# A two-block transformer kernel: its modulation products issued four at a time, one in each 32-column quarter of the array

## The chip, the cores and the metric

The kernel runs on one core of a Trainium2 chip. Its time is the device time of one execution in microseconds (us); the median of several runs is compared. Five engines work side by side, each through its own instructions in order, and wait for one another through semaphores: TensorE (PE in the profile; its weight loads are shown apart as PEld), VectorE (DVE), ScalarE (ACT), GpSimd (POOL) and SyncE (SP), which here only issues DMA transfers. Some DMAs are issued from ScalarE's queue as well.

## The reference

Two model blocks run one after the other on 256 tokens of 1024 channels, two layers each. The first is a mixer of four branches (a recurrence, a latent attention, a convolution, a cross attention), merged with gates. The second is a block with feed-forward, attention and feed-forward in each layer. Each of its six sublayers is modulated: two conditioning vectors `c` and `c_ctx`, one for each of two token streams, are taken through silu and multiplied with a large matrix, which gives nine rows of 1024 values a layer (shift, scale and gate of each of three sublayers):

```python
h = modulate(rms_norm(x, g_pre), shift, scale)    # h * (1 + scale) + shift
x = x + weight * gate * rms_norm(sublayer(h), g_post)
# shift, scale, gate: parts of  silu(c) @ w_mod + b_mod,  w_mod [1024, 9 * 1024] a layer
```

The modulation rows depend on `c` and `c_ctx` alone, so they can be worked out at any time before the sublayer that reads them. All arithmetic is in float32. The large products are made of three passes in float32r (a 12-bit high and a low part of each operand); the modulation products are plain float32.

## The kernel before

All weights are streamed from DRAM once, in tiles of 128 x 1024 float32 (512 KB). Each tile comes into a pool `wr` of four buffers (line 241) by a DMA on SyncE's queue. `wload` (lines 180 to 192) issues the DMA, lets ScalarE cast the tile to its high part `wh` (line 177) and VectorE subtract to get its low part `wl` (line 178); these two have three buffers each. A `wr` buffer is free again once VectorE has read it. TensorE then multiplies the two parts with the activations: 24 matmuls a weight tile (8 pieces of the contraction, 3 passes), of 256 columns in the first block and of 512 in most of the second. All matmuls are recorded under line 169, all transposes under line 172, so they are told apart by tiles: `ac`, `rw` and `sm` are PSUM banks of the products, `md` is the one bank of the modulation.

The modulation is worked out by a generator, `mods` (lines 1155 to 1201), that runs in the background: `wload` ends with `tick` (line 216), which takes each background generator one step further, that is, up to its next `yield`. In layer 1 of the first block `mods` makes the rows of the first sublayer at one step a tick (line 360). In the second block it makes the other five sublayers at one step every second tick (line 1227, `MODS_TICKS`). The attention adds ticks of its own at each pair of heads, six in the first token stream and two in the second (`HEAD_TICKS`, line 57), between the scores of that pair and the values of the one before; there is no weight tile between these, so modulation steps follow one another.

A sublayer takes six blocks of 512 columns, each over a contraction of 1024. A block is four steps and a fifth. In each of the four, one tile of the modulation matrix is fetched into a `wr` buffer, used by TensorE as it is, without cast, and given back:

```python
for i in range(4):
    ...
    for k in range(2):
        kk = 2 * i + k
        g = 32 * (kk % 4)
        self.mm(ps[g : g + 32], self.cs[:, kk], raw[:, 512 * k : 512 * k + 512], kk < 4, kk >= 4)
    yield
```

The stationary operand `cs` is 128 x 32 (two conditioning vectors and 30 columns of zeros), so a product fills one 32-column quarter of the array and leaves its result in 32 partitions of the bank. Piece `kk` of the contraction goes to quarter `kk % 4`: a step with even `i` uses quarters 0 and 1, one with odd `i` quarters 2 and 3. Each product is recorded as two matmuls and two weight loads, so a step is four matmul records. In the fifth step ScalarE copies the bank into a `wr` buffer (line 1173), and two small DMAs carry the rows to DRAM; after six blocks the four quarters are added and the result is brought into the form that the sublayers read (lines 1178 to 1201).

The framework draws up the order of each engine's instructions when the kernel is built: by the order in which they were issued, but work that it holds ready can be put ahead of work that it expects to wait. Buffers of a pool are given out from those that are free.

Of the kernel before, what the change touches and what calls it, by code (L numbers as in the profile page):

```python
# [9 lines left out]
F32 = mybir.dt.float32  # L10
# [6 lines left out]
PSUM = bass.MemoryType.PSUM  # L17
# [4 lines left out]
S = 256  # L22
W = 512
T = 512
# [28 lines left out]
RWKV_STEPS = ((2, 1), (2, 1))           # by layer and duo  # L53
RWKV_GAPS = (2, 3, 3, 2, 1, 4)
CONV_STEPS, CONV_GAP, XQ_GAP, MLA_GAPS = 3, 2, 1, (2, 1)
MODS_TICKS = 2                          # ticks a step
HEAD_TICKS = (6, 2)                     # ticks at a pair of heads, by stream
HEADS_AHEAD = (0, 1)                    # pairs whose values wait, by stream
EVS = 5                                 # buffers
COLS = ((0, 1), (1, 2), (3, 2), (5, 2), (7, 1))     # row tiles that are transposed at a time  # L60
# [99 lines left out]
class Build:  # L160
# [6 lines left out]
    # -- building stones --  # L167
# [6 lines left out]
    def split(self, h, l, src, eng=None):  # L174
        """src = h + l exactly, h and l with the 12 significant bits of float32r"""
        nc = self.nc
        nc.scalar.copy(h, src)  # L177
        (eng or nc.vector).tensor_tensor(out=l, in0=src, in1=h.bitcast(F32), op=ALU.subtract)  # L178
# [15 lines left out]
    def gemm(self, out, sa, sb, KT):  # L194
        """out = sum over k of a^T b, three float32r passes; sa(k), sb(k) give (high, low)"""
# [7 lines left out]
    def rsqrt(self, out, in_, n):  # L203
        """out = in_ ** -0.5 (exact to float32 rounding), [p, n]"""
        p = in_.shape[0]
        self.nc.gpsimd.tensor_tensor(out=out, in0=in_, in1=self.mhalf[:p, :n], op=ALU.pow)  # L206
# [9 lines left out]
    def tick(self):  # L216
        """a step of the work that is spread over the stream of weights"""
# [17 lines left out]
    # -- the whole --  # L235
    def build(self):
        nc, tc, ap = self.nc, self.tc, self.ap
        with ExitStack() as st:
# [15 lines left out]
            # what the end of the first block needs on the one side, the rest of it and then the second on the other  # L254
# [7 lines left out]
    # ================= first block =================  # L262
    def first(self, fin, st):
# [3 lines left out]
        self.ts = fin.enter_context(tc.tile_pool(name="ts", bufs=4))     # a few columns  # L267
        p1 = self.p1 = pool("p1", 1)
        self.f4 = fin.enter_context(tc.tile_pool(name="f4", bufs=7))     # [128, 1024]
# [9 lines left out]
        self.t1 = pool("t1", 2)     # [128, 256] scratch  # L279
        self.t2 = pool("t2", 2)     # [128, 512] scratch  # L280
        self.d2 = pool("d2", 16)    # [128, 512], four heads of the recurrence
        self.d4 = pool("d4", 5)     # [128, 1024]
        self.rp = pool("rp", 1)     # its diagonal blocks
# [5 lines left out]
    def trig(self):  # L289
        """cos and sin of positions * inv_freq, [token, tile, 16]"""  # L290
# [27 lines left out]
        # the quotient may be off by one either way  # L318
# [63 lines left out]
    def params(self, l):  # L382
        """the small weights of a layer"""
# [4 lines left out]
        # halves and the like, worked out on the chip  # L388
# [21 lines left out]
    def wtile(self, ps):  # L410
        """the next 128 columns of w_in"""
# [8 lines left out]
    def move(self, ps, h, lo, kt, k0, K, lhs, n=512):  # L420
        """ps += rows k0.. of the weights (n columns each), streamed; lhs(k) the stationary parts"""
# [7 lines left out]
    def memkv(self, l):  # L429
        """k^T [d, head, m] and v [m, (head d)] of the memory tokens"""  # L430
# [29 lines left out]
    def gated(self, n):  # L460
        """silu(gate) times the branch, in two parts: the operands of the output projection"""
# [16 lines left out]
    # -- RWKV --  # L478
    def shift(self, p, mu, omu, out):
        """out = (1 - mu) * p + mu * p_prev, tokens along the free dimension"""  # L480
# [27 lines left out]
    def rwkv(self, duo, k0, r, v0):  # L508
        """Four heads at once. By channel: [(head in pair, d), pair, token]; by token: [(chunk & 1, token in chunk),
        (pair, chunk >> 1, head in pair), .]. A system (head and chunk) fills a 64 x 64 corner of the array."""  # L510
# [8 lines left out]
        # every system: head, chunk, pair; its halves of the partitions by channel and by token, its 64 columns in  # L519
        # the order (pair, chunk), (head, pair, chunk >> 1) and (chunk & 1, pair, chunk >> 1). Two systems whose  # L520
        # operands lie in different halves of the partitions never share a bank.
# [6 lines left out]
        # decay and learning rate  # L528
# [26 lines left out]
        # kk = k * k_k, normalised per head  # L555
# [24 lines left out]
        # scaled operands  # L580
# [18 lines left out]
        # inverses of the 16x16 diagonal blocks, row after row: a row of a block goes to the partitions of its block  # L599
# [26 lines left out]
        # by token  # L626
# [15 lines left out]
        # bonus  # L642
# [12 lines left out]
        # blocks of 32, then of 64  # L655
# [29 lines left out]
        # u = ta S + c0 for the state S of a chunk, and S' = e (m S + cs)  # L685
# [46 lines left out]
        # the rows: rk v + rb u, and r S  # L732
# [9 lines left out]
        # there is no state before the first chunk  # L742
# [19 lines left out]
        # group norm over a head, and the bonus  # L762
# [27 lines left out]
    # -- convolution --  # L790
# [31 lines left out]
    def norm_stats(self, src, eps, n=1):  # L822
        """mean and (variance + eps) ** -0.5 of the rows; src a list of [128, <=512]"""
# [11 lines left out]
    def conv_norm(self):  # L835
        """layer norm over the channels, then silu: self.cx becomes 2 silu(.)"""
# [24 lines left out]
    # -- attention over the memory --  # L861
# [835 lines left out]
```

## Time and profile before

| what | before |
|---|---|
| median of 3 runs | 2757.94 us (2756.73 to 2766.02) |
| span of the profiled execution | 2758.4 us |
| TensorE busy in it | 2691.4 us (98%) |
| VectorE, ScalarE, GpSimd busy | 1539.3, 1145.3, 219.5 us |
| mean granted clock of TensorE | 0.991 |
| matmul records of the modulation, and the time in which at least one ran | 576, 158.0 us |
| tiles of the modulation matrix | 144 of 512 KB |
| mean DMA rate | 140 GB/s |

The span runs from the first to the last instruction of the profiled execution; its difference to the median, 0.5 us, is well inside what the runs differ by. Busy time of a group is the time in which at least one of its instructions ran, so matmuls that run beside each other are counted once, while "mean ns of one" is the length of each.

### The profile page before, as it was taken

Reading aid. Unit: us, or ns where it says so; the run is one execution under the profiler, and the core shown is the slowest. Engines: PE = TensorE matmul, PEld = TensorE weight load, DVE = VectorE, ACT = ScalarE, POOL = GpSimd, SP = SyncE. Lnnn points to the kernel's source line nnn. Section 1 sums busy time; section 2 is a strip of 40 time slices with the busy share of each in tenths; the row PEclk is TensorE's granted clock in tenths of the full one; section 3 lists DMA queues with packets and bytes.
Section 4 is the critical chain, followed back from the end, with each engine's and each line's share of the span. In section 5 each row is a group of like instructions: output and inputs, shape, how many; then the busy total and the mean of one; then the engine's idle time right before and its main releaser. Section 6 shows DMA issues by size and latency. Waiting matters only on the chain.

```text
span 2758.4 us, 43028 instructions
## 1 busy us (share of the span) xinstructions
PE 2691.4 (98%) x17138; PEld 2183.3 (79%) x17138; DVE 1539.3 (56%) x2646; ACT 1145.3 (42%) x1964; POOL 219.5 (8%) x240
## 2 busy tenths in 40 slices
PE   8999999999999999999999999999999999999999
PEld 7888998787999777777755777777777777765897
DVE  7997667897666533345635442335533334744656
ACT  5465455445545322234436422224422224535445
POOL 1121110112011000000102000000000000110000
PEclk9999999999999999999999999999999999999999
DMA  6344466546366534434433344444444343434565
GB/s 204 95 129 131 150 199 212 161 141 183 116 185 204 168 119 130 128 111 127 120 108 111 115 119 127 124 121 118 123 130 122 117 131 116 131 123 135 168 183 151
DMA packets 134906, 385.07 MB, mean 140 GB/s; under 512 B 38481, under 2 KB 42385, under 8 KB 134577
## 3 DMA queue, kind: packets, MB, share of 16 engines
q1 hardware_dynamic: 121216, 379.25, 45.7%
q10 hardware_dynamic: 13488, 3.07, 0.5%
q8 instruction: 135, 2.21, 0.3%
q14 instruction: 67, 0.54, 0.1%
HBM read 379.43 MB, written 2.83 MB: 139 GB/s over the span
## 4 chain that ended last, share of the span: by engine, by line
PE 86%; DVE 8%; ACT 2%; issue 2%; DMA 1%; POOL 1%; ACTq 0%; DVEq 0%; SPq 0%; POOLq 0%
PE ac L169 42%; PE rw L169 27%; PE sm L169 10%; PE md L169 5%; PE sm L172 2%; DVE wl L178 2%; DVE br L817 2%; DMA wr<-in_win 1%; DVE br L1352 0%; ACT wh L177 0%; PE rw L172 0%; POOL rso L206 0%; POOL rs L206 0%; DVE u L1345 0%; DVE u L1263 0%
## 5 line engine op out<-in xcount | busy, mean ns | idle before, releaser
L178 DVE TENSOR_TENSOR wl<-wr,wh 128x1024 fp32r<-128x1024 f32 (+2 forms) x547 | 699.5, 1280 | 507.9 <-ACT wh L177 506.1
L177 ACT CAST wh<-wr 128x1024 fp32r<-128x1024 f32 (+2 forms) x547 | 568.2, 1039 | 953.6 <-PE ac L169 439.2
L169 PE MATMUL rw<-blk,wh 128*128 128x512 f32 (+1 forms) x1712 | 461.6, 354 | 1.3 <-DVE blk L1282 1.1
L169 PE MATMUL ac<-blk,wh 128*128 128x512 f32 (+1 forms) x1728 | 460.8, 352 | 0.0
L169 PE MATMUL ac<-xth,wh 128*128 128x256 f32 x1248 | 357.7, 287 | 5.7 <-ACT wh L177 5.2
L169 PEld LDWEIGHTS rw<-blk,wh 128*128 128x128 f32 x1712 | 302.4, 191 | 71.2 <-ACT wh L177 27.7
L169 PEld LDWEIGHTS ac<-blk,wh 128*128 128x128 f32 x1728 | 305.4, 190 | 58.5 <-ACT wh L177 14.3
L169 PE MATMUL ac<-xth,wl 128*128 128x256 f32 x1248 | 350.0, 281 | 1.2 <-DVE wl L178 1.2
L169 PE MATMUL ac<-xtl,wh 128*128 128x256 f32 x1248 | 349.9, 281 | 0.1
L169 PE MATMUL rw<-blk,wl 128*128 128x512 f32 (+1 forms) x856 | 301.0, 352 | 4.2 <-DVE wl L178 4.2
L169 PE MATMUL ac<-blk,wl 128*128 128x512 f32 (+1 forms) x864 | 301.9, 349 | 1.8 <-DVE wl L178 1.8
L169 PEld LDWEIGHTS ac<-xth,wh 128*128 128x128 f32 x1248 | 236.2, 189 | 22.2 <-issue 10.7
L169 PEld LDWEIGHTS ac<-xth,wl 128*128 128x128 f32 x1248 | 236.1, 189 | 3.8 <-DVE wl L178 2.2
L169 PEld LDWEIGHTS ac<-xtl,wh 128*128 128x128 f32 x1248 | 236.4, 190 | 2.5 <-issue 1.6
L178 DVE TENSOR_TENSOR al<-blk,ah 128x512 fp32r<-128x512 f32 (+1 forms) x170 | 104.9, 621 | 146.8 <-ACT ah L177 146.6
L169 PEld LDWEIGHTS rw<-blk,wl 128*128 128x128 f32 x856 | 163.1, 191 | 26.8 <-DVE wl L178 4.4
L169 PEld LDWEIGHTS ac<-blk,wl 128*128 128x128 f32 x864 | 164.1, 190 | 23.4 <-DVE wl L178 2.2
L177 ACT CAST ah<-blk 128x512 fp32r<-128x512 f32 (+1 forms) x170 | 95.4, 564 | 201.1 <-PE rw L169 102.6
L169 PE MATMUL md<-wr,cs 128*32 128x512 f32 x576 | 158.0, 612 | 3.7 <-DMA wr<-in_wmod 2.2
L1396 DVE SCALAR_TENSOR_TENSOR blk<-u,rw 128x512 f32<-128x512 f32 (+1 forms) x66 | 39.5, 598 | 160.9 <-PE rw L169 160.8
L206 POOL TENSOR_TENSOR rso<-rso,mhalf 128x1 f32<-128x1 f32 x20 | 11.0, 551 | 1420.7 <-DVE rso L1347 1420.7
L169 PE MATMUL ac<-f,wh 128*128 128x256 f32 x640 | 117.0, 282 | 0.0
(417 smaller groups left out, 4112.1 us busy)
## 6 DMA issues: line engine op xcount, KB each, us to landing
wr<-in_w SPq DMA_DIRECT2D x264, 512.0 KB
wr<-in_win SPq DMA_DIRECT2D x187, 512.0 KB
wr<-in_wmod SPq DMA_DIRECT2D x144, 512.0 KB
wr<-in_wo SPq DMA_DIRECT2D x32, 512.0 KB
wr<-in_wout SPq DMA_DIRECT2D x32, 512.0 KB
wr<-in_wkv SPq DMA_DIRECT2D x16, 512.0 KB
gate<-gd SPq DMA_DIRECT2D x10, 512.0 KB
blk<-in_rpb SPq DMA_DIRECT2D x48, 64.0 KB
```

What stands on the lines that cost most here:

```text
L169: self.nc.tensor.matmul(out, a, b, start=start, stop=stop, skip_group_check=True)
L172: self.nc.tensor.transpose(out, a, self.ident[:n, :n])
L177: nc.scalar.copy(h, src)
L178: (eng or nc.vector).tensor_tensor(out=l, in0=src, in1=h.bitcast(F32), op=ALU.subtract)
L206: self.nc.gpsimd.tensor_tensor(out=out, in0=in_, in1=self.mhalf[:p, :n], op=ALU.pow)
L817: V.scalar_tensor_tensor(out=acc, in0=hp[:, j : j + 256], scalar=w(j), in1=acc, op0=ALU.mult, op1=ALU.add)
L1396: V.scalar_tensor_tensor(out=a(u // 2), in0=t, scalar=0.5, in1=pu, op0=ALU.mult, op1=ALU.mult)
```

## The change

A block's four steps with one tile each become two rounds of two steps. In the first step of a round both tiles of the round are fetched and nothing else is done; in the second, four products are issued one after the other, one in each quarter of the array. The number of steps in a block (five), of tiles, of products, of records and of bytes stays as it was, and so does every product's quarter and place in the accumulation. The rest of the diff takes out comments.

```diff
-                for i in range(4):
+                for i in range(0, 4, 2):
                     u = 4 * blk + i
-                    raw = self.wr.tile([128, 1024], F32, name="wr")
-                    nc.sync.dma_start(out=raw, in_=ap["wmod"][l, :, 1024 * u : 1024 * u + 1024])
-                    for k in range(2):
-                        kk = 2 * i + k
-                        g = 32 * (kk % 4)
-                        self.mm(ps[g : g + 32], self.cs[:, kk], raw[:, 512 * k : 512 * k + 512], kk < 4, kk >= 4)
+                    raw = [self.wr.tile([128, 1024], F32, name="wr") for _ in range(2)]
+                    for j in range(2):
+                        nc.sync.dma_start(out=raw[j], in_=ap["wmod"][l, :, 1024 * (u + j) : 1024 * (u + j) + 1024])
+                    yield
+
+                    for k in range(4):
+                        self.mm(ps[32 * k : 32 * k + 32], self.cs[:, 2 * i + k],
+                                raw[k // 2][:, 512 * (k % 2) : 512 * (k % 2) + 512], i == 0, i == 2)
                     yield
```

## Rows read from the trace of the kernel before

**Rows 1.** The page: span, busy time of each engine, chain that ended last.

```profile
span 2758.4 us, 43028 instructions
PE 2691.4 (98%) x17138; PEld 2183.3 (79%) x17138; DVE 1539.3 (56%) x2646; ACT 1145.3 (42%) x1964; POOL 219.5 (8%) x240
...
PE 86%; DVE 8%; ACT 2%; issue 2%; DMA 1%; POOL 1%; ACTq 0%; DVEq 0%; SPq 0%; POOLq 0%
PE ac L169 42%; PE rw L169 27%; PE sm L169 10%; PE md L169 5%; PE sm L172 2%; DVE wl L178 2%; DVE br L817 2%; DMA wr<-in_win 1%; DVE br L1352 0%; ACT wh L177 0%; PE rw L172 0%; POOL rso L206 0%; POOL rs L206 0%; DVE u L1345 0%; DVE u L1263 0%
```

**Rows 2.** Stretches: length, busy PE, PEld, DVE, ACT, POOL, clock, DMA share, GB/s.

```profile
500.00:670.00 170.00, 163.41 (x1601) 128.36 (x1601) 148.86 (x339) 77.50 (x156) 34.17 (x47) 1.00 0.52 158
...
1408.00:1510.00 102.00, 99.46 (x458) 49.24 (x458) 55.13 (x220) 55.09 (x148) 19.32 (x15) 0.93 0.40 121
...
1600.00:2370.00 770.00, 767.34 (x3399) 590.53 (x3398) 306.20 (x385) 239.38 (x352) 8.54 (x14) 1.00 0.41 122
```

**Rows 3.** The same for `md` alone: PE, PEld, DVE, ACT, clock, DMA; sum.

```profile
500.00:670.00 170.00, 27.33 (x96) 3.72 (x96) 0.00 (x0) 3.52 (x6) 1.00 0.52 158
...
1408.00:1510.00 102.00, 17.77 (x73) 2.61 (x73) 0.19 (x1) 2.36 (x4) 0.93 0.40 121
...
2455.00:2515.00 60.00, 15.43 (x56) 1.97 (x56) 0.00 (x0) 2.38 (x4) 0.94 0.37 116
sum 1780.00, PE 158.95 PEld 22.04 DVE 0.77 ACT 21.02; mean PE 22.71 PEld 3.15 DVE 0.11 ACT 3.00
```

**Rows 4.** DMA issues of the page: tiles of the modulation matrix.

```profile
wr<-in_wmod SPq DMA_DIRECT2D x144, 512.0 KB
```

**Rows 5.** Chain of 1600 to 1700 us: start, length, what, how many.

```profile
1604.67 0.98 PE md L169 x4
1605.65 5.67 PE rw L169 x24
1611.33 5.44 PE ac L169 x24
```

**Rows 6.** Chain of 1400 to 1600 us, the attention of layer 0: modulation pieces.

```profile
1416.26 1.85 PE md L169 x16
...
1436.17 1.00 PE md L169 x8
1437.75 0.97 PE md L169 x2
...
1442.52 0.98 PE md L169 x4
...
1452.00 0.99 PE md L169 x6
```

**Rows 7.** Whole span, waits: who for whom, us, times, longest.

```profile
PE sm L172 <- DVE u L1263: 5.4, 4, 3.4
...
PE md L169 <- DMA wr<-in_wmod: 2.2, 2, 1.2
```

**Rows 8.** Chain of 500 to 670 us by line, the first block's stretch.

```profile
by line: PE ac L169 29.0%; DVE br L817 14.7%; PE md L169 9.2%; PE rw L169 8.3%; DVE wl L178 6.2%; PE sm L169 4.1%; issue 3.9%; DMA wr<-in_win 3.2%; DMA ms<-wr 2.2%; PE rw L172 1.7%; ACTq L1183 1.5%; ACT wh L177 1.2%; DVE d L595 1.1%; POOL r
```

**Rows 9.** Timeline of ScalarE, 1646 to 1682 us: start, length, idle before.

```profile
1658.30 1.05 ACT L177 CAST wh<-wr 128x1024 fp32r<-128x1024 f32 x1 [5.11 <-PE rw L169]
```

**Rows 10.** Timeline of SyncE, 600 to 650 us: two weight loads issued.

```profile
612.92 4.76 SPq L185 DMA_DIRECT2D wr<-in_wukv  x2
```

**Rows 11.** Timeline of ScalarE, 600 to 622 us: the cast that waits for them.

```profile
617.10 1.05 ACT L177 CAST wh<-wr 128x1024 fp32r<-128x1024 f32 x1 [3.41 <-DMA wr<-in_wukv]
```

**Rows 12.** Groups of the page: subtraction and cast of the weight tiles.

```profile
L178 DVE TENSOR_TENSOR wl<-wr,wh 128x1024 fp32r<-128x1024 f32 (+2 forms) x547 | 699.5, 1280 | 507.9 <-ACT wh L177 506.1
L177 ACT CAST wh<-wr 128x1024 fp32r<-128x1024 f32 (+2 forms) x547 | 568.2, 1039 | 953.6 <-PE ac L169 439.2
```

**Rows 13.** A stretch of the attention of layer 0 (columns of rows 2).

```profile
1421.90:1435.40 13.50, 12.73 (x36) 6.07 (x36) 6.44 (x27) 4.33 (x11) 1.78 (x1) 0.50 0.21 71
```

## The prediction

> **What bounds the kernel now.** I read the page first, for which engine sets the end: TensorE is busy for 98% of a span of 2758.4 us, and 86% of the chain that ended last is TensorE's; the modulation products alone are 5% of that chain, some 138 us [rows 1]. Then the stretches, for where this holds: in the second block's feed-forward parts TensorE is busy for 767 of 770 us and no other engine for more than 306 [rows 2]. There, a microsecond less of TensorE is a microsecond less of time. In the first block's stretch with modulation (500 to 670 us) VectorE is busy for 149 of 170 us beside TensorE's 163, so there are two near-bounds [rows 2]. In the attention TensorE is busy for 99 of 102 us [rows 2], but with the modulation steps as filling between the scores of one pair of heads and the values of another. So three kinds of stretch have to be costed apart.
>
> The modulation's share of each [rows 3]: 158.95 us in sum, of which 27.33 in the first block, 17.77 and 15.43 in the two attentions. A step is four records, so these are 24, 18 and 14 steps (one of the 73 records of the first attention is a transpose); of the 144 in all [rows 4], 88 are left for the feed-forward parts, the output projections and the attention's own input products.
>
> **What a group of products costs.** This is the point on which the change rests, and the trace of before answers it, since the built order has in places put steps side by side [rows 6]. One product alone (x2 records) takes 0.97 us, two in two quarters (x4) 0.98, three (x6) 0.99, four in four quarters (x8) 1.00, and two rounds of four (x16) 1.85. So four cost 0.03 us more than one: the quarters run beside each other in full. Around a group there is a second cost, in the products of the main stream: the 24 matmuls after a modulation step take 5.67 us where 24 others take 5.44 [rows 5], so a group also costs 0.23 us that isn't in its own rows. A group thus costs 0.98 + 0.23 = 1.21 us in the feed-forward parts, and one of four 1.00 + 0.23 = 1.23 us.
>
> The Trainium skill speaks to both, in sentences that the sum does without. On the 0.23 us: TensorEngine Tiling, section Tiling Modes, says that a change of the tiling mode drains the engine; half as many groups are half as many changes, by that rule and by the rows alike. On the overlap: TensorE: Matmul & The Clock Gate, section Part 3, reports 2.38 times the speed for three column tiles of 512 columns; the trace disagrees, with 0.99 us for three against 0.97 for one, which is 2.9 times.
>
> **The change part by part.**
>
> *Feed-forward parts and projections, 88 steps.* 44 pairs of steps become 44 groups of four: each pair saves 2 x 1.21 - 1.23 = 1.19 us, 52 us in all. From this go the steps that stand where TensorE waits anyway: at the ends of sublayers its transposes wait for the normalised rows of VectorE (four waits, 5.4 us [rows 7]), and a modulation step there fills a wait. I count six such steps, three pairs, 3.6 us. What is left is 48 us.
>
> *First block, 24 steps.* The modulation is 9.2% of the chain of this stretch [rows 8], 15.6 of its 170 us, against 27.33 us of busy time: 57% of it is on the path. The gain in busy time is 12 x (2 x 0.98 - 1.00) = 11.5 us; 57% of that is 6.6 us. What speaks against it is the order of the loads. Both tiles of a round now stand ahead of the next weight tile in SyncE's queue, where one stood. At a DMA share of 0.41 the DMA engines moved 122 GB/s [rows 2], so some 298 GB/s when all are at work, and a tile of 512 KB is an estimated 1.8 us of them. The weight loads are the nearest to late here: a cast waited 3.41 us for a weight tile whose load had been issued 4.2 us earlier [rows 10, 11]. If each of 12 rounds delays a weight tile by a whole tile, 21.6 us are lost; if none, nothing. I take a loss of 2 us, near the lower end, since a load is late only in few places (3.2% of the chain [rows 8], 5.4 us), and so a net gain of 5 us, with ends of -15 and +11.5.
>
> *The two attentions, 32 steps.* 33.2 us of busy time become 16 groups of 1.00 us, so TensorE has 17 us less to do. How much of it is time depends on the softmax that these steps cover: a pair of heads gives its scores, three steps follow, then the values of the pair before. With 1.5 groups in place of three steps the cover is some 1.5 us thinner. TensorE is busy for all but 2.5 us of 102 [rows 2], so it isn't far ahead of its inputs, nor is it far behind. No row shows what the wait would be without that cover: between 0 and 17 us of gain. I take 6, a third: TensorE is nearly full now, so the filling fits the wait closely, and what is cut from it returns largely as waiting.
>
> *The clock.* In the attention TensorE's granted clock fell to 0.50, its lower level of 1.2 GHz, from 1421.9 to 1435.4 us [rows 13], after a round of 16 modulation records at 1416 us and a piece of scores. At half speed these 13.5 us hold what 6.8 us would hold at 2.4 GHz. Whether the fall comes earlier, later or not at all with other work in its place can't be read from the rows: plus or minus 7 us, and I take 0.
>
> *Added waits and buffers.* A group of four now waits for two tiles, and behind it on TensorE stands the whole main stream. Before, modulation products waited for their tile twice, 2.2 us in all [rows 7]. The tiles are now fetched two ticks ahead of their use, which is earlier than before, so I cost this at nothing. The price is that a round holds two of the four `wr` buffers for two ticks longer. What covers it in the feed-forward parts: the casts there wait for TensorE to give back a `wh` buffer (5.11 us [rows 9]), not for a load, so each weight tile lies in its buffer some 5 us before it is cast, and its cast and subtraction (1.04 and 1.28 us [rows 12]) are done two weight tiles, 11 us, before TensorE needs them. Two buffers for the weight stream still give one load in 5.44 us, and a load took 4.2 us under traffic [rows 10, 11]. Were that cover gone, each group would expose load, cast and subtraction, 6.5 us, less the 5.44 us of one weight tile's products: 1.1 us.
>
> *The number of steps* is as before, so no sublayer gets its modulation later, and copies and small DMAs stay.
>
> **The sum.** 48 + 5 + 6 = 59 us off the profiled execution's 2758.4 us, to 2699; the median of the runs is 0.5 us lower, so I say 2698 us.
>
> **The rivals.**
>
> *TensorE is the path everywhere.* All of 52, 11.5 and 17 us come off: 2677 us. For it: 86% of the chain is TensorE's. Against it: VectorE's 149 of 170 us in the first block.
>
> *The gain is given back in the first block and the attention.* There is no gain in the attention, and the first block loses 15 us to late weight tiles: 2758 - 48 + 15 = 2725 us. For it: VectorE and loads are on the chain already [rows 8]. Against it: the loads wait in few places.
>
> *The four overlap worse when they are the rule.* A group of four lies between 1.00 us and two groups of two, 1.96 us, if four streams share something that two don't. A quarter of the way, 1.24 us, 72 groups lose 17 us: 2698 + 17 = 2715 us. Against it stand the x6 and x8 pieces [rows 6]. The Trainium skill's figure from TensorE: Matmul & The Clock Gate, section Part 3, if it held for four quarters in proportion, would be an estimated 1.23 us.
>
> *The groups are torn apart.* The built order may put other work between products of a group, as it did where a step of two shows as two pieces of x2, of which one stands in [rows 6]. If all became pairs, there would be 144 groups again: 2758 us.
>
> *The buffers run dry, and it is slower.* Where rounds hold two buffers each and one is fetched before the one ahead of it is used up, the weight stream has less than the buffers it needs, and each of the 72 groups exposes 1.1 us, 79 us in all: 2698 + 79 = 2777 us. It decides from 0.85 us a group. Against it: casts in the feed-forward parts wait for TensorE with 5 us to spare [rows 9].
>
> **How the numbers follow.** The forecast (2680 to 2710 us) has a chance of 0.60, TensorE as the path everywhere 0.10, the gain given back 0.16, a poorer overlap 0.05, groups torn apart 0.04, dry buffers 0.05. A difference under 0.3%, 8 us, is about what a measurement of this kernel can tell from no change. Faster by more has 0.60 + 0.10 + 0.16 + 0.05 = 0.91, the same 0.04, slower 0.05. The range of 8 in 10 takes in the forecast, the upper end of the gain and the smaller half of what could be given back: 2677 to 2718 us.
>
> **What would show it.** In the profile after, the modulation's busy time should be some 75 us in place of 158.95, in pieces of x8 at 1.00 us, and the feed-forward stretch of 770 us shorter by 28 us (24 pairs of 1.19). The first block's stretch should be within 15 us of 170, and the chain in it should have VectorE and loads with larger shares. In the attention, waits of TensorE for the softmax should be new. Pieces of x4 in number, or pieces of x8 longer than 1.05 us, would make the prediction wrong at its root; casts that wait for weight loads in the feed-forward parts would mean that the buffers ran dry.

## The result, and the profile after

The changed kernel takes 2718.42 us (median of 4 runs) against 2761.8 us of the kernel before, timed beside it: a ratio of 0.9845 (95% interval 0.9822 to 0.9867). Timed again in a later session it was 2713.23 against 2757.52 us, 0.9832 (0.9811 to 0.9852). So it is faster by some 43 to 46 us. I had forecast 60 and a range that ended at 2718 us; the first median lies 0.4 us outside it. The direction and the price of a group were right; a quarter of the gain was missing.

The page of the changed kernel, in the order of [rows 1]:

```profile
span 2721.0 us, 43032 instructions
PE 2644.5 (97%) x17138; PEld 2188.4 (80%) x17138; DVE 1537.4 (57%) x2646; ACT 1145.1 (42%) x1964; POOL 223.2 (8%) x240
...
PE 84%; DVE 8%; ACT 2%; DMA 2%; issue 2%; POOL 1%; SPq 0%; ACTq 0%; DVEq 0%; POOLq 0%
PE ac L169 43%; PE rw L169 26%; PE sm L169 9%; PE md L169 3%; DVE wl L178 2%; PE sm L172 2%; DVE br L817 2%; ACT wh L177 1%; DVE br L1354 1%; DMA wr<-in_win 1%; DMA wr<-in_wmod 0%; PE rw L172 0%; DVE u L1347 0%; POOL rso L206 0%; POOL rs L206 0%
```

The modulation's share of the chain went from 5% to 3%, TensorE's busy time from 2691.4 to 2644.5 us. In a feed-forward part the chain shows the new groups (start, length, what, how many records); [rows 5] is the same place before:

```profile
1651.55 1.00 PE md L169 x8
1652.54 5.67 PE rw L169 x24
1658.21 5.44 PE ac L169 x24
1663.65 5.44 PE rw L169 x24
1669.10 5.44 PE ac L169 x24
1674.53 0.99 PE md L169 x8
```

Four products in 1.00 us, and 0.23 us in the matmuls behind them, once in four weight tiles in place of once in two. Now four stretches that begin and end with the casts of the same weight tiles, before and after: the first block's part with modulation, the attention of layer 0, that of layer 1, and a feed-forward part. The columns are those of [rows 2]. Before:

```profile
503.60:677.00 173.40, 166.81 (x1632) 131.45 (x1631) 151.71 (x342) 76.97 (x154) 38.22 (x49) 1.00 0.53 160
1368.90:1482.70 113.80, 112.29 (x488) 63.11 (x488) 46.84 (x168) 48.93 (x111) 13.95 (x9) 0.94 0.37 113
2416.90:2520.80 103.90, 98.67 (x454) 54.80 (x453) 46.27 (x164) 45.30 (x104) 12.95 (x8) 0.95 0.38 118
1593.70:1911.60 317.90, 317.90 (x1376) 244.94 (x1375) 117.24 (x136) 89.62 (x121) 0.00 (x0) 1.00 0.42 123
```

After:

```profile
505.80:680.00 174.20, 161.01 (x1631) 133.88 (x1631) 151.10 (x342) 76.06 (x155) 40.61 (x49) 0.98 0.50 161
1361.00:1473.90 112.90, 111.35 (x488) 62.99 (x488) 47.18 (x168) 49.05 (x112) 13.74 (x9) 0.94 0.36 113
2380.60:2484.30 103.70, 98.56 (x457) 55.08 (x449) 46.30 (x164) 45.17 (x105) 12.74 (x8) 0.93 0.38 119
1584.90:1890.80 305.90, 305.90 (x1372) 244.40 (x1372) 117.12 (x136) 89.63 (x120) 0.00 (x0) 1.00 0.41 126
```

The same for the modulation's matmuls alone (length, busy time and records, clock, DMA share, GB/s), before and then after:

```profile
503.60:677.00 173.40, 27.33 (x96) 1.00 0.53 160
1368.90:1482.70 113.80, 19.63 (x80) 0.94 0.37 113
2416.90:2520.80 103.90, 18.58 (x68) 0.95 0.38 118
1593.70:1911.60 317.90, 19.99 (x76) 1.00 0.42 123
```

```profile
505.80:680.00 174.20, 16.70 (x96) 0.98 0.50 161
1361.00:1473.90 112.90, 18.63 (x80) 0.94 0.36 113
2380.60:2484.30 103.70, 17.20 (x72) 0.93 0.38 119
1584.90:1890.80 305.90, 9.59 (x72) 1.00 0.41 126
```

The feed-forward part went from 317.9 to 305.9 us, TensorE busy for all of it in both. The other three stretches took 173.4, 113.8 and 103.9 us before and take 174.2, 112.9 and 103.7 us now: next to nothing was gained there. In the two attentions the modulation is busy for nearly as long as before (18.63 and 17.20 us, 19.63 and 18.58 before), though each product now has three others to run beside. The chain from 1400 to 1500 us shows why (compare [rows 6]):

```profile
1418.81 1.84 PE md L169 x2
...
1426.20 1.04 PE md L169 x6
1429.22 0.97 PE md L169 x2
1431.91 0.98 PE md L169 x2
1433.73 0.98 PE md L169 x4
1438.97 0.97 PE md L169 x2
1443.10 0.99 PE md L169 x8
1448.14 0.99 PE md L169 x6
```

The groups are torn: one product, other work, then the other three, or one, one and two. A piece costs about 0.98 us whether it holds one product or four, so a group torn in two costs as much as two steps did. Over the whole kernel there are 96 pieces of products where 72 groups would do; before there were 147. Groups are torn outside the attention too: in the five places of the table's last row the modulation's products are busy for 22.4 us (29.3 before), though their 100 records would make 12.5 groups of 1.00 us.

The table gives the time between casts of the same weight tiles in two profiles of each kernel (the second ones are from the experiments):

| part | before | changed |
|---|---|---|
| first block with modulation, and the part behind it | 372.0, 370.7 | 372.5, 372.1 |
| feed-forward, layer 0, first | 354.4, 354.4 | 341.3, 341.3 |
| feed-forward, layer 0, second | 317.9, 317.9 | 305.9, 305.9 |
| feed-forward, layer 1, first | 317.9, 317.9 | 305.9, 305.9 |
| attention, layer 0 | 113.8, 113.9 | 112.9, 113.2 |
| attention, layer 1, with what follows | 128.4, 126.8 | 127.4, 126.7 |
| ends of sublayers and input products, five places in sum | 437.3, 435.6 | 436.3, 428.8 |

### The profile page after: what moved, and what is told of

Read it like the earlier page. It is cut to its first block, busy times and chain, and to the rows that moved or that the text cites. A ratio compares the mean times of both kernels' runs of the same rounds, so it can differ in the third digit from the quotient of the medians.

```text
span 2721.0 us, 43032 instructions
## 1 busy us (share of the span) xinstructions
PE 2644.5 (97%) x17138; PEld 2188.4 (80%) x17138; DVE 1537.4 (57%) x2646; ACT 1145.1 (42%) x1964; POOL 223.2 (8%) x240
## 4 chain that ended last, share of the span: by engine, by line
PE 84%; DVE 8%; ACT 2%; DMA 2%; issue 2%; POOL 1%; SPq 0%; ACTq 0%; DVEq 0%; POOLq 0%
PE ac L169 43%; PE rw L169 26%; PE sm L169 9%; PE md L169 3%; DVE wl L178 2%; PE sm L172 2%; DVE br L817 2%; ACT wh L177 1%; DVE br L1354 1%; DMA wr<-in_win 1%; DMA wr<-in_wmod 0%; PE rw L172 0%; DVE u L1347 0%; POOL rso L206 0%; POOL rs L206 0%
## 5 line engine op out<-in xcount | busy, mean ns | idle before, releaser
L817 DVE SCALAR_TENSOR_TENSOR br<-hp,pv,br 128x256 f32<-128x256 f32 x240 | 114.1, 511 | 0.9
```

The lines of the kernel that those rows point to most:

```text
L817: V.scalar_tensor_tensor(out=acc, in0=hp[:, j : j + 256], scalar=w(j), in1=acc, op0=ALU.mult, op1=ALU.add)
```

## The experiments

Two theories stood for the attention. "Torn": the missing gain is the tearing of the groups. "Cover": the softmax sets the pace there, so that less filling only means more waiting. For the first block: "VectorE", "late tiles" (two modulation tiles stand ahead of each weight tile and hold two of four buffers) and "clock".

### Groups kept whole

The first product issued is now the one that needs the round's second tile, and the other three are tied to it, so that they stand right behind it in TensorE's order.

```diff
-                    for k in range(4):
-                        self.mm(ps[32 * k : 32 * k + 32], self.cs[:, 2 * i + k],
-                                raw[k // 2][:, 512 * (k % 2) : 512 * (k % 2) + 512], i == 0, i == 2)
+                    with ExitStack() as one:
+                        for k in (2, 3, 0, 1):
+                            ins = nc.tensor.matmul(ps[32 * k : 32 * k + 32], self.cs[:, 2 * i + k],
+                                                   raw[k // 2][:, 512 * (k % 2) : 512 * (k % 2) + 512], start=i == 0,
+                                                   stop=i == 2, skip_group_check=True)
+                            if k == 2:
+                                one.enter_context(self.tc.issue_after(ins.ins))
+                                one.enter_context(self.tc.high_priority())
```

> The changed kernel with each group of four kept whole: the first product issued waits for the round's second tile, and the other three are queued right behind it ahead of other work. In the changed kernel's profile the modulation is busy for 18.85 us in the first attention's 100 us and 15.43 us in the second's 60 us, no less than before the change, in pieces of x2, x4 and x6. Theory 'torn': the missing gain in the attention is the tearing. Then the modulation's busy time falls to some 9 and 7 us there, about 72 pieces of x8 in all, and the time falls by 10 to 17 us from the changed kernel's 2718 to 2701 to 2708 us. Theory 'cover': the softmax sets the attention's pace. Then the busy time falls as well, TensorE's waits for the softmax grow by as much, and the time stays at 2718 us, within 4 us.

Measured: 2700.09 us, ratio 0.9796 (0.9773 to 0.9819), some 10 to 13 us less than the changed kernel. The two attentions, same bounds as above, all engines and then the modulation alone:

```profile
1351.50:1452.40 100.90, 98.76 (x488) 59.82 (x487) 47.15 (x168) 48.89 (x112) 13.69 (x9) 1.00 0.41 128
2360.60:2451.60 91.00, 85.99 (x431) 51.00 (x431) 45.12 (x164) 42.96 (x101) 12.88 (x8) 0.96 0.41 130
```

```profile
1351.50:1452.40 100.90, 10.45 (x80) 1.00 0.41 128
2360.60:2451.60 91.00, 10.46 (x72) 0.96 0.41 130
```

They are 12.0 and 12.7 us shorter than in the changed kernel, and some 4 us of the second come back behind it (27.4 us in place of 23.7 or 22.8): TensorE is busy for 27.1 us of that stretch, since work that stood ahead of its first cast now stands behind it (28 products with `pt` in place of 20, 28 transposes of `u` in place of 16). TensorE's waits for the softmax (on `pt`) hardly grew: 6.5 us in the whole kernel, against 5.7 with torn groups. "Torn" holds; "cover" falls. Part of the gain is the clock's: in the changed kernel and the kernel before (two profiles of each) TensorE ran at 1.2 GHz for 13.7 us near the start of the attention of layer 0, behind the 16-record piece and a piece of scores, and with whole groups it didn't; in that of layer 1 it did for 6.8 us in place of 13.7. That whole groups are what keeps the fall away is not shown (see the first block in the form of before).

### The control: pairs kept together in the kernel before

The same tie around the two products of a step, in the kernel before:

```diff
-                    for k in range(2):
-                        kk = 2 * i + k
-                        g = 32 * (kk % 4)
-                        self.mm(ps[g : g + 32], self.cs[:, kk], raw[:, 512 * k : 512 * k + 512], kk < 4, kk >= 4)
+                    with ExitStack() as one:
+                        for k in range(2):
+                            kk = 2 * i + k
+                            g = 32 * (kk % 4)
+                            ins = nc.tensor.matmul(ps[g : g + 32], self.cs[:, kk], raw[:, 512 * k : 512 * k + 512],
+                                                   start=kk < 4, stop=kk >= 4, skip_group_check=True)
+                            if k == 0:
+                                one.enter_context(self.tc.issue_after(ins.ins))
+                                one.enter_context(self.tc.high_priority())
```

> The kernel before, with the two products of each step kept together in the same way as in the run with whole groups: the second is queued right behind the first ahead of other work. It is the control for that run, in which the time fell by some 13 us from the changed kernel. Theory 'groups of four': it was the number of groups that fell, so this kernel stays at the time of before, 2758 us within 5 us. Theory 'order': putting the modulation's products ahead of other work is what helped in the attention, so this kernel gains 8 us or more there, 2750 us or less.

Measured: 2754.41 us, ratio 0.9977 (0.9964 to 0.9991). The two attentions:

```profile
1366.10:1478.80 112.70, 110.24 (x488) 62.78 (x487) 46.87 (x168) 48.89 (x111) 14.17 (x9) 0.94 0.38 114
2412.20:2515.00 102.80, 97.56 (x449) 54.55 (x449) 45.41 (x163) 45.12 (x104) 12.21 (x8) 0.95 0.39 119
```

They take 1.1 us less each than before. So order alone is worth some 6 us in the kernel (2 to 10 by the interval) and 2 in the attentions. What whole groups gave beyond that is their number, and the lower clock that is not there: the 13.7 us at 1.2 GHz stand in this profile too.

### The first block in the form of before

```diff
+                for i in range(4 if (l, sub) == (0, 0) else 0):
+                    u = 4 * blk + i
+                    raw = self.wr.tile([128, 1024], F32, name="wr")
+                    nc.sync.dma_start(out=raw, in_=ap["wmod"][l, :, 1024 * u : 1024 * u + 1024])
+                    for k in range(2):
+                        kk = 2 * i + k
+                        g = 32 * (kk % 4)
+                        self.mm(ps[g : g + 32], self.cs[:, kk], raw[:, 512 * k : 512 * k + 512], kk < 4, kk >= 4)
+                    yield
-                for i in range(0, 4, 2):
+                for i in range(0, 0 if (l, sub) == (0, 0) else 4, 2):
```

> The changed kernel, with the first sublayer's modulation (the one made in the first block) in the form of before, one tile a step and two products at a time; the other five sublayers in the new form. Theory 'no gain there': the first block's stretch is set by VectorE and by late weight tiles, so the time is that of the changed kernel, 2718 us within 4 us. Theory 'the gain is there but was hidden by the profile's clock': the time is 5 to 11 us above the changed kernel, 2723 to 2729 us. A time below 2714 us would say that the new form costs time in the first block.

Measured: 2713.15 us, 0.9841 (0.9825 to 0.9858), the same as the changed kernel. The part of the first block takes 371.6 us. The new form gains nothing there that these runs can tell, and their intervals are some 5 us to either side. Its profile has a second finding, in the attention of layer 0:

```profile
1355.60:1462.70 107.10, 105.57 (x488) 60.60 (x487) 47.08 (x168) 49.10 (x112) 13.76 (x9) 1.00 0.38 119
```

It has the same torn groups but no fall of the clock, and takes 107.1 us, between 113 (torn, with the fall) and 100.9 (whole, without it). So of the 12 us that whole groups gain there in the profiles, some 6 are pieces and 6 are the clock. TensorE's order in this attention is the changed kernel's (the same tiles, record for record), so the order in it does not by itself decide whether the clock falls.

The same with the tie of whole groups in the steps that keep the new form, so in all but the first block (both diffs above together):

> Groups of four kept whole in the second block, and the first block's modulation in the form of before. From casts of the same weight tiles, the first block's part with modulation and the part behind it took 372.0 us before, 372.5 and 372.1 us with the changed kernel, 370.2 us with whole groups and 371.6 us with the old form there. If the first block gains nothing from groups of four, the time equals that of the run with whole groups, 2700 us within 4 us; if it gains 5 us or more, 2705 us or above; if the old form is better there (fewer falls of the clock), below 2696 us.

Measured: 2699.71 us, 0.9784 (0.9768 to 0.98), with whole groups everywhere 0.9796. Again no difference, though in this profile the first block's part took 375.2 us, the longest of the five profiles that have the form of before there (369.9 to 375.2). This is the fastest version measured, by no more than the intervals allow.

### Loads in two steps

```diff
-                    raw = [self.wr.tile([128, 1024], F32, name="wr") for _ in range(2)]
+                    raw = []
                     for j in range(2):
+                        raw.append(self.wr.tile([128, 1024], F32, name="wr"))
...
-                    yield
+                        if j == 0:
+                            yield
```

> Groups kept whole as in the run before it, and the two tiles of a round fetched in two steps: the first tile alone, then the second together with the four products. So one modulation tile stands ahead of each weight tile in SyncE's queue, as before the change, and tiles are held for a shorter time. In the changed kernel ScalarE waited 27.1 us for weight tiles in the first block's stretch (9.9 before). Theory 'late tiles': these waits fall to some 10 us, and the first block's stretch of 500 to 690 us gets 5 to 10 us shorter than in the run with whole groups. Theory 'VectorE': the waits fall but the stretch keeps its length within 2 us. Against both: TensorE waits longer for the second tile, and the time is above that of the run with whole groups.

Measured: 2706.41 us, 0.981 (0.9791 to 0.9829), no better than 0.9796 with both loads in one step. ScalarE's waits for these weight tiles fell to 20.2 us only, and the first block's part took 378.6 us with TensorE at 1.2 GHz for 24 us of it, so this profile alone doesn't part "late tiles" from the rest. Neither theory's length came (5 to 10 us shorter, or within 2 us).

### A fifth buffer in the first block

```diff
-EVS = 5
+EVS = 3
...
+        self.wq = pool("wq", 1)
...
-        pts = self.twice(tag="e2", bufs=4)
+        pts = self.twice(tag="e2", bufs=3)
...
-                    raw = [self.wr.tile([128, 1024], F32, name="wr") for _ in range(2)]
+                    own = (l, sub) == (0, 0)
+                    raw = [self.wq.tile([128, 1024], F32, name="wq") if own and j else
+                           self.wr.tile([128, 1024], F32, name="wr") for j in range(2)]
```

> Groups of four kept whole, and in the first block the second modulation tile of each round has a buffer of its own beside the four of the weight stream (room for it comes from two scratch pools, with 3 buffers in place of 5 and 4). With whole groups the first block's part with modulation and the part behind it took 370.2 us between casts of the same weight tiles, ScalarE waited there 29.2 us for weight tiles, TensorE's busy time was 9 us lower than before and the time of the part the same within 2 us; 12 more groups made it 15 us longer. Theory 'buffers': a weight load starts late since a round holds two of four buffers. Then ScalarE's waits for weight tiles fall below 15 us, TensorE's idle time shrinks by 5 us or more, and the part takes 365 us or less. Theory 'other engines': the waits may fall, but the part keeps 370 us within 2 us. Layer 0 up to the same cast (445 us) shows whether the smaller scratch pools cost anything themselves.

Measured: 2701.02 us, 0.9799 (0.9783 to 0.9814). ScalarE's waits for weight tiles in the first block: before, in the changed kernel, with whole groups, and then with the fifth buffer as well (who for whom: us, times, longest):

```profile
ACT wh L177 <- DMA wr<-in_win: 9.9, 7, 3.8
```

```profile
ACT wh L177 <- DMA wr<-in_win: 27.1, 8, 7.5
```

```profile
ACT wh L177 <- DMA wr<-in_win: 29.2, 12, 8.3
```

```profile
ACT wh L177 <- DMA wr<-in_win: 16.1, 11, 3.8
```

The tiles came earlier, and the part kept its length to 0.1 us: 370.3 us with and without. In this profile TensorE waits there for VectorE's results instead. So "late tiles" alone is not the bound, as far as the smaller scratch pools, from which the room came, cost nothing in the same part. The stretch from the cast of weight tile 66 to that of 120 took 157.5 us (157.3 with whole groups alone), but the part ahead of it 285.8 in place of 282.2 us, with TensorE at 1.2 GHz for 10.2 us in it (6.8 us at 46 us, 3.4 us at 179 us) in place of 3.4. Half of the 6.8 us more is 3.4 us, an estimate that leaves the pools little; that they bring the falls is not excluded.

### More products in the first block

In the first sublayer's modulation the first round's products were issued three times over (with whole groups):

```diff
+                    for _ in range(3 if (l, sub, i) == (0, 0, 0) else 1):
                       with ExitStack() as one:
```

> Groups kept whole, and in the first sublayer's modulation (made in the first block) the first round's four products issued three times over, which leaves the same sum: 12 more groups there, 10 to 12 us more of TensorE in a stretch in which VectorE is busy for about 150 of 168 to 176 us whatever the form. Theory 'VectorE and the loads set this stretch': TensorE has room, the stretch grows by less than 5 us, and the time is within 5 us of 2700 us. Theory 'TensorE sets it and the clock took the gain': the stretch grows by 10 us or more, less what fewer falls of the clock give back (1.7 us for each 3.4 us at the lower clock).

Measured: 2712.36 us, 0.9834 (0.9821 to 0.9848). The first block's part, from the kernel before, the changed kernel, the kernel with whole groups and this one (columns of [rows 2]):

```profile
503.60:875.60 372.00, 364.32 (x3654) 321.28 (x3653) 286.84 (x544) 178.20 (x321) 62.20 (x68) 1.00 0.54 163
```

```profile
505.80:878.30 372.50, 357.85 (x3650) 323.31 (x3650) 286.04 (x544) 177.23 (x320) 64.59 (x68) 0.99 0.53 163
```

```profile
501.90:872.20 370.30, 354.96 (x3651) 322.95 (x3651) 286.26 (x544) 177.03 (x321) 63.19 (x68) 0.99 0.53 164
```

```profile
503.60:889.30 385.70, 369.21 (x3748) 329.78 (x3749) 286.64 (x544) 177.11 (x321) 64.61 (x68) 0.98 0.51 157
```

From the third row to the fourth the part grew by 15.4 us for 14.3 us more of TensorE's busy time, and its idle time stayed at 15.3 and 16.5 us. So TensorE has no room there, against "VectorE". But the change, which takes work away, didn't shorten it: the kernel before has 364.3 us busy in 372.0, the changed one 357.9 in 372.5. The modulation's own busy time fell by 10.6 us, TensorE's by 6.5, since the clock fell at 511 and 651 us (3.4 us each at 1.2 GHz; before, in neither or one of the two places), and the idle time rose by 7.

The two results come closer when the lower clock is taken out. In this part TensorE ran at 1.2 GHz for 0 and 3.4 us in the two profiles of the kernel before, 6.8 us in both of the changed kernel, 10.2 us here with whole groups and 17.1 us with the added products. If half of that time is taken off, an estimate and rather too much where TensorE was idle, 372.0 and 369.0 us are left before, 369 us in the changed kernel, 365 to 368 us in the five profiles with whole groups, and 377 us with the added products: some 10 us for 12 groups. The idle time goes with the form: 6 to 8 us in the five profiles with one tile a step there, 14 to 17 us in all profiles with rounds of two, with a fifth buffer or without.

### Half of the groups

The products of the first round of each block were left out (half of the modulation sum is not computed), so those of the second begin their sums.

```diff
-                    for k in range(4):
+                    for k in range(4 if i else 0):
                         self.mm(ps[32 * k : 32 * k + 32], self.cs[:, 2 * i + k],
-                                raw[k // 2][:, 512 * (k % 2) : 512 * (k % 2) + 512], i == 0, i == 2)
+                                raw[k // 2][:, 512 * (k % 2) : 512 * (k % 2) + 512], True, True)
```

> The changed kernel without the products of the first round of each block, so 36 of 72 groups are left out (half of the modulation sum is not computed); all tiles are still fetched. This prices a group of four in the whole program. Theory 'on the path everywhere': 36 groups of 1.23 us, 44 us less than the changed kernel, 2674 us. Theory 'on the path in the feed-forward parts only': 22 groups, 27 us less, 2691 us, with the attention's and the first block's stretches as long as in the changed kernel.

Measured: 2675.81 us, 0.9711 (0.9696 to 0.9726), 37 us less than the changed kernel as first timed (0.9845 - 0.9711 of 2758.6 us) and 33 us less than as timed again (0.9832), between the two expectations. The feed-forward parts give 6.1, 4.9 and 4.9 us for 5, 4 and 4 groups left out, 1.22 us each, as priced; the rest is spread over the first block (369.0 us in place of 372.5 and 372.1), the attentions (105.3 and 99.1 us in place of 112.9 and 103.7) and the ends of sublayers (426.9 us in sum in place of 436.3 and 428.8). In the last two several groups were torn and cost more than one piece.

### More and fewer ticks in the attention

Both with whole groups:

```diff
-HEAD_TICKS = (6, 2)
+HEAD_TICKS = (12, 4)
```

> Groups kept whole, and twice as many ticks at each pair of heads (12 and 4 in place of 6 and 2), so that the attention holds as many microseconds of modulation as before the change; the other parts hold fewer. Theory 'cover' (the softmax needs 3 us of other work at each pair of heads): the time falls by 5 to 15 us from the run with whole groups at the old ticks (2700 us), since the work moved in is free there. Theory 'no cover needed' (in that run TensorE's waits for the softmax stayed at 2.1 and 3.7 us in the two attentions with half the filling): each group costs its 1.00 us wherever it stands, and the time stays at 2700 us, within 5 us.

Measured: 2723.28 us, 0.9882 (0.9866 to 0.9897). The attention of layer 0 with what follows took 241.8 us in place of 212.6:

```profile
1349.50:1591.30 241.80, 228.84 (x1151) 146.05 (x1151) 108.46 (x323) 109.26 (x258) 30.10 (x28) 0.94 0.45 140
```

TensorE is busy 22 us longer there (13 of them modulation, the rest mostly the clock, 0.94 in place of 0.99) and idle 7 us longer. More filling is not free there, against "cover"; but the time left the 2695 to 2705 us of "no cover needed" as well, and the loss was larger than either theory said. The 13.7 us at 1.2 GHz near the start of this attention are back, though its groups are whole.

And in the other direction:

```diff
-HEAD_TICKS = (6, 2)
+HEAD_TICKS = (2, 2)
```

> Groups kept whole, and a third of the ticks at the pairs of heads of the first token stream (2 and 2 in place of 6 and 2), so each such pair holds half a group of modulation. Theory 'cover': TensorE's waits for the softmax grow by 1 to 2 us a pair, 12 to 24 us in the two attentions, and the time rises to 2710 us or more. Theory 'no cover needed': the waits grow by less than 4 us and the time stays within 6 us of 2700 us, unless the modulation of the last sublayers then comes late, which would show as one long wait of TensorE at the end of the second attention.

Measured: 2724.52 us, 0.9875 (0.986 to 0.989). The attention of layer 0 with what follows took 214.0 us against 212.6, with 2.1 us of waits for the softmax, though between its first and last product with `pt` only 32 modulation records stand in place of 56. The loss is at the end, as the expectation allowed: the last sublayer's modulation came late. One line of TensorE's waits (us, times, longest), and the stretch behind it:

```profile
PE md L172 <- DMA wr<-gd: 22.3, 3, 17.2
```

```profile
2509.00:2533.00 24.00, 6.53 (x31) 6.43 (x32) 8.38 (x18) 6.73 (x12) 0.00 (x0) 0.50 0.48 138
```

### Both kernels again

The changed kernel and the kernel before, unaltered.

> The changed kernel unaltered, timed beside the next three on one chip. Expected 2718 us within 5 us. It settles two sizes: how far it lies from the kernel with whole groups (2700 us in an earlier call; expected difference 10 to 18 us), and how much of its time is the state of TensorE's clock: in its first profile TensorE ran 71 us at the lower clock, against 52 us in the kernel before. If the lower clock is a lasting effect of the change, the second profile shows 65 us or more again; if it varies from run to run, anything between 40 and 85.

Measured: 2713.23 us, 0.9832 (0.9811 to 0.9852); 67 us at the lower clock.

> The kernel before unaltered, for a second profile of it. In its first profile TensorE ran 52 us of the span at the lower clock, in two profiles of the changed kernel 71 and 67 us. If the change itself lowers the clock, this profile shows 45 to 55 us again, with none at 510 and 650 us in the first block; if the lower clock varies by as much as that from run to run, it may show 65 us. The feed-forward stretches between the same weight tiles should repeat to 0.1 us: 354.4, 317.9 and 317.9 us.

Measured: 2754.94 us; 53 us at the lower clock, with a fall of 3.4 us at 507 us and none at 650. The feed-forward parts repeat to 0.1 us. So 52 and 53 us before, 71 and 67 us after: in the profiles some 16 us more at half speed, which is 8 us. Timed runs have their granted clock on record too, and over them the difference is smaller: 0.989 in the mean of nine runs of the changed kernel (0.986 to 0.994), 0.991 in that of 42 runs of the kernel before (0.988 to 0.994). That is an estimated 57 and 51 us at half speed, so the clock cost the medians some 3 us, not 8.

## Why the prediction was right or wrong

*The price of a group was right.* Four products in 1.00 us and 0.23 us behind them give, for the first feed-forward part, 22 x 1.21 - 11 x 1.23 = 13.1 us, and 13.1 were measured; for the other two 19 x 1.21 - 9 x 1.23 = 11.9, and 12.0 were measured. The Trainium skill's figure of 2.38 for three column tiles, from TensorE: Matmul & The Clock Gate, section Part 3, did not hold in this kernel: the pieces of the kernel before gave 2.9 times for three [rows 6], and the whole program bears out 3.9 times for four (4 x 0.97 / 1.00).

*What was wrong* is where else that price would be saved. The step that failed is that outside the feed-forward parts, too, pairs of steps become whole groups whose price comes off the time: the groups were torn, and where they were not, waits and the lower clock took the place of what was saved. Against the sum of 48 + 5 + 6 = 59 us (52 less 3.6 is 48.4, written as 48), the table of parts gives 41:

- Feed-forward parts and projections, 48 us. Of the 88 steps 60 lie in the three feed-forward parts and gave 37.1 us, as worked out. The other 28, at the ends of sublayers and in the attention's input products, were put at 17 us less 3.6 for steps that fill waits, so 13 us; the five places gave 1.0 us in one pair of profiles and 6.8 in the other. Over all eight profiles that have the new form there with every product and the same ticks, they take 428.8 to 438.8 us, 435.3 in the mean, and 435.6 to 437.3 in three profiles of the form of before: some 1 us. The groups are torn there too: the modulation's products are busy for 29.3 us before, 22.4 us in the changed kernel and 12.8 us with whole groups. But whole groups, too, leave 434.5 us. In their profile TensorE is idle there for 24.4 us in place of 17.3, most of the 7 us in waits for the normalised and modulated rows of a sublayer (`u` and `blk`, 14 us in place of 8), and it runs at 1.2 GHz for 24 us in place of 14, an estimated 5 us lost. I had counted six steps as filling waits; far more of them did, and the clock took a part of what was saved.
- The attentions, 6 us (0 to 17). They gave 1.4 us, with the stretch behind the second. The step "33.2 us of busy time become 16 groups of 1.00 us" failed: busy time stayed, since the groups were torn. I had the tearing as a rival, at 0.04 and for all groups or none, though the trace had its signs: steps of two in two pieces, and pieces of x6, most of them in the attention. The reason I gave for taking only a third, a softmax that waits, was wrong: with whole groups these waits hardly grew (6.5 us in the kernel in place of 5.7) and the attentions got 12.0 and 12.7 us shorter, a good part of it by the clock.
- The first block, 5 us (-15 to +11.5). It gave -1. Late weight tiles, which I gave as the risk, did come (27.1 us of ScalarE's waits in place of 9.9), but a fifth buffer removed half of them and moved nothing. TensorE's busy time fell by 6.5 us and its idle time rose by 7; the lower clock took some 3 us of what the products saved. Which wait makes the idle time is open.
- The clock, taken as 0 (plus or minus 7). It cost some 8 us in the profiles, an estimated 3 us over all timed runs.

*The buffers* were right for the feed-forward parts: TensorE is busy in 305.90 of 305.90 us, so no weight tile came late. Had groups been whole, 0.9796 of the 2757.94 us would be 2702 us; the forecast was 2698. That this comes so close is in part luck: in the profile with whole groups the attentions gave 22 us in place of the 6 forecast, part of them by the clock, and made up for the 11 that were missing at the ends of sublayers and the 4 in the first block.

## What to carry to other kernels

Products that fill only a part of the array can be costed before they are changed, if the trace somewhere has two, three or four of them side by side: take the length of such pieces and the extra time of the work behind them. But a group that is issued together is not yet a group in the order that is built: where the group is filler for other work, look at its pieces in the trace, and tie it together if it was torn. And price a saving stretch by stretch: in the changed kernel it counted in full where the engine was never idle, and hardly anywhere else.

## What the runs showed of the hardware that I had not expected

- TensorE's clock fell to 1.2 GHz where it was hardly idle: in the kernel before it was busy for 13.65 of the 13.8 us ahead of the fall and for 12.73 of the 13.5 us at the lower clock [rows 13]. It came at the same place in two profiles each of two kernels and in the control with pairs, and was absent in one profile with the same order of TensorE's work in this attention. So neither idle time nor the order in this stretch explains it, and its cause is open. The time of the attention of layer 0 differed by 6 us with it (113 and 107.1 us, both with torn groups).
- The feed-forward parts repeat to 0.1 us in two profiles of a kernel, taken in different sessions, so that a group's price of 1.2 us can be read from a single profile, while the runs' whole time varies by 8 to 18 us within a session.

The row ahead of the fall, with the columns of [rows 2]:

```profile
1408.00:1421.80 13.80, 13.65 (x56) 7.25 (x54) 6.16 (x27) 5.60 (x13) 1.57 (x1) 1.00 0.51 160
```
